# State-space decays from running sums that a DMA spreads over all partitions, in place of two TensorE products for each chunk and group

## The chip, the cores and the metric

The kernel runs on one core of one Trainium2 chip. The metric is the device time of one execution in microseconds (us). The time before is the median of three executions.

## The reference

Two layers of a decoder trunk are computed for one sequence of 1024 positions with width 1024. Each layer normalises the input, multiplies it by one input projection, feeds four branches (HGRN2, retention, Mamba-2 state space, gated linear attention), and adds the projected, gated outputs back. The change is in the state-space branch (SSD), which has 8 heads in 2 groups of 4:

```python
def chunked_scalar_decay(q, k, v, log_a):
...
    def step(state, inp):
        qc, kc, vc, ac = inp
        cum = jnp.cumsum(ac, axis=-1)
        rel = jnp.where(causal, cum[..., :, None] - cum[..., None, :], -jnp.inf)
        scores = jnp.einsum('bhtd,bhsd->bhts', qc, kc) * jnp.exp(rel)
        o = (jnp.einsum('bhts,bhsv->bhtv', scores, vc)
             + jnp.einsum('bhtd,bhdv->bhtv', qc * jnp.exp(cum)[..., None], state))
...
def ssd_branch(z_in, xbc_in, dt_in, conv_w, conv_b, dt_bias, a_log, d_skip, norm_g):
...
    dt = jax.nn.softplus(dt_in.astype(jnp.float32) + dt_bias.astype(jnp.float32)).transpose(0, 2, 1)
    a = -jnp.exp(a_log.astype(jnp.float32))
...
    y = chunked_scalar_decay(group_to_heads(cmat), group_to_heads(bmat),
                             xh * dt[..., None], dt * a[None, :, None])
```

What matters here is `exp(rel)`: for each chunk and head, a matrix over pairs of positions (s, t) with the exponential of the sum of the log decays between s and t.

## The kernel before, in words

The kernel cuts the sequence into 8 chunks of 128 positions (`NC` = 8, where the reference uses 64; the result is the same). One layer runs through its branches one after another: HGRN2 (4 heads), gated linear attention (2 pairs of heads), SSD (2 groups), retention (4 heads). Dense projections, in and out, are split in a high and a low part and take three TensorE matmuls each. They are generators, and `fill(ns)` pulls matmuls from them whenever a branch yields a number of nanoseconds: so the in-order stream of TensorE (PE) holds the small products of a branch with pieces of dense projections between them. This order is the order in which the program is written. The order on VectorE (DVE), ScalarE (ACT), GpSimd (POOL) and the DMA queue of SyncE (SP) is made by a scheduler, and each of them runs its own list strictly in order. Weights come as 256 KB slices (tile `raw`, 2 buffers) by DMAs on SP's queue; ACT rounds each to its high part (`whi`, L402), DVE makes the low part (`wlo`, L403), 4 buffers of each.

For SSD, `ssd_steps` works once in each layer, in two parts. The first computes the step sizes `dt` and the log decays `la` (128 positions of a chunk on the partitions, 8 chunks x 8 heads = 64 columns). The second, run after the HGRN2 heads, makes on PE three products of `la` with constant triangular or full matrices (L915 to L917) into one PSUM tile, takes their exponentials (L919, tile `dx`), and splits `la` into a high part `lah` and a rest `lal` (L922, L924).

`ssd_mix(l, g, ...)` works through the 8 chunks of a group; it runs four times (2 layers x 2 groups). The scores of 4 chunks at a time are 4 products on PE (`scores`, L994), masked on DVE into `M` (L997). The decay matrices of a chunk, 128 x 512 for 4 heads, come in three steps that run ahead of use:

- `factors(c)`: POOL multiplies the constant triangle `upper` by the column of `la` of each head, once for `lah` and once for `lal` (L1003, two tiles `lv`).
- `decays(c, lvs)`: PE multiplies both by the constant `after_r` into one PSUM tile `sc` (L1012, two matmuls of 512 columns), ACT takes the exponential into a tile `A` (L1014), DVE multiplies it by `M` (L1015).
- `weighted(c)`: POOL makes three scaled copies of the chunk's input (`xdt`, `xw`, `xd`, L1028).

Then PE makes the chunk's output `po` (L1061 from `A`, L1064 from the carried state; one PSUM buffer) and its state update (L1067); DVE adds them up (L1070 to L1086), ACT takes the squares (L1089). After 4 chunks POOL computes the inverse root (L269, L271), DVE scales (L1097), and PE transposes the result for the output projection (`to_feature_major`, L521). `factors` is called two chunks ahead and `decays` one chunk ahead. The tiles `lv`, `A` and `M` come from one pool of 5 buffers, `mid` (names `b2` and `lv`).

While a group runs, the dense work between its chunks is an output projection (L1118), then the convolution's projections of the next group (L417 to L419, with L946, L947 on ACT and L950 on DVE) in group 0, or the rotary projections of the retention branch (L464 to L467, with L836 on ACT and L840 to L845 on DVE and POOL) in group 1.

Of the kernel before, what the change touches and what calls it, by code (L numbers as in the profile page):

```python
# [11 lines left out]
F32 = mybir.dt.float32  # L12
F32R = mybir.dt.float32r
# [3 lines left out]
AF = mybir.ActivationFunctionType  # L17
ALU = mybir.AluOpType
MUL, ADD, SUB = ALU.mult, ALU.add, ALU.subtract
PSUM = bass.MemoryType.PSUM  # L20

P = 128
# [144 lines left out]
def hybrid_trunk(ctx, nc, tc, t_in, out, gamma_c):  # L167
    vec, act, gp, pe = nc.vector, nc.scalar, nc.gpsimd, nc.tensor
    SL = 512

    cst = ctx.enter_context(tc.tile_pool(name="cst", bufs=1))
    wp = ctx.enter_context(tc.tile_pool(name="wp", bufs=4))
    big = ctx.enter_context(tc.tile_pool(name="big", bufs=11))
    mid = ctx.enter_context(tc.tile_pool(name="mid", bufs=5))
    yp = ctx.enter_context(tc.tile_pool(name="yp", bufs=4))
    sml = ctx.enter_context(tc.tile_pool(name="sml", bufs=4))
    pp = ctx.enter_context(tc.tile_pool(name="pp", bufs=4, space=PSUM))
    pm = ctx.enter_context(tc.tile_pool(name="pm", bufs=1, space=PSUM))

    seq = [0]  # L180

    def nm(s):
        seq[0] += 1
        return f"{s}_{seq[0]}"
# [4 lines left out]
    def mid_t(n=512):  # L189
        return mid.tile([P, 512], F32, tag="b2", name=nm("b2"))[:, :n]  # L190

    def sm_t(tag, n, bufs=4, w=None):
        return sml.tile([P, w or n], F32, tag=tag, bufs=bufs, name=nm(tag))[:, :n]
# [4 lines left out]
    def ps_mix(tag, bufs=1):  # L198
        return pm.tile([P, 512], F32, tag=tag, bufs=bufs, name=nm(tag))
# [46 lines left out]
        return cols[:, o : o + n] if j is None else cols[:, o + j : o + j + 1]  # L246

    ident, upper, ones = k_("ident"), k_("upper"), k_("ones")
    after_r = cst.tile([P, P], F32R, name="after_r")
    vec.tensor_tensor(after_r, ones, upper, SUB)  # L250
    after = after_r.bitcast(F32)

    xs = cst.tile([P, NT, D], F32, name="xs")
    hh = [cst.tile([P, KT, 512], F32R, name=f"hh{i}") for i in range(2)]
# [19 lines left out]
    def bc(ap, shape):  # L274
        return ap.to_broadcast(shape)
# [603 lines left out]
    def ssd_steps(l, dl, st):  # L879
# [7 lines left out]
        def t64(tag):  # L887
            return sm_t(tag, 64, bufs=1)
# [19 lines left out]
        dt = t64("dt")  # L908
# [6 lines left out]
        pe.matmul(ps[:, 0:64], upper, la, start=True, stop=True)  # L915
        pe.matmul(ps[:, 64:128], after, la, start=True, stop=True)
        pe.matmul(ps[:, 128:192], ones, la, start=True, stop=True)  # L917
        ex = sm_t("dx", 192, bufs=1)
        act.activation(ex, ps[:, 0:192], AF.Exp)  # L919

        lah = sml.tile([P, 64], F32R, tag="lah", bufs=1, name=nm("lah"))
        vec.tensor_copy(lah, la)  # L922
        lal = t64("lal")
        vec.tensor_tensor(lal, la, lah.bitcast(F32), SUB)  # L924
        w = t64("dw")
        vec.tensor_tensor(w, ex[:, 64:128], dt, MUL)

        def v3_(a):
            return a.rearrange("p (c h) -> p c h", c=NC)

        st.update(dt=v3_(dt), la=(v3_(lah.bitcast(F32)), v3_(lal)), ec=v3_(ex[:, 0:64]), w=v3_(w),
                  dec=v3_(ex[:, 128:192]), dsk=dsk)

    def conv(l, ch, u, name):
# [50 lines left out]
    def ssd_mix(l, g, u, st, between):  # L985
# [11 lines left out]
            vec.tensor_tensor(M[half], ps.rearrange("p (c t) -> p c t", c=4), bc(upper.unsqueeze(1), [P, 4, P]), MUL)  # L997

        def factors(c):
            lvs = []  # L1000
            for part in st["la"]:
                lv = mid.tile([P, 512], F32R, tag="b2", name=nm("lv"))
                gp.tensor_tensor(lv.rearrange("p (h t) -> p h t", h=4), bc(upper.unsqueeze(1), [P, 4, P]),  # L1003
                                 bc(part[:, c, hs].unsqueeze(2), [P, 4, P]), MUL)
                lvs.append(lv)
            return lvs

        def decays(c, lvs):

            pl = ps_mix("sc", 2)  # L1010
            for i_, lv in enumerate(lvs):
                pe.matmul(pl, after_r, lv, start=(i_ == 0), stop=(i_ == 1))  # L1012
            A = mid_t().rearrange("p (h t) -> p h t", h=4)
            act.activation(A, pl.rearrange("p (h t) -> p h t", h=4), AF.Exp)  # L1014
            vec.tensor_tensor(A, A, bc(M[c // 4][:, c % 4, :].unsqueeze(1), [P, 4, P]), MUL)  # L1015
            return A

# [259 lines left out]
    for l in range(DEPTH):  # L1277
# [4 lines left out]
        st = {}  # L1282
# [176 lines left out]
```

## Time and profile before

| | |
|---|---|
| median of three executions | 2104.41 us (2104.26 to 2104.89) |
| the profiled execution, its own time | 2105.0 us |
| its span in the profile | 2103.2 us |
| mean granted TensorE clock | 0.994 |
| DMA traffic | 115.72 MB, 55 GB/s over the span |

The profile is of one execution. Its views give, for each engine, busy time and what ended each idle time (the waits), instructions in order of time (the timeline), groups by line, and busy time by stretch (windows). In the timeline a row has the start in us from the span's start, the duration of the merged instructions, engine, line, operation, tiles and count, and in brackets the idle time before it and what ended it. Matmuls are pipelined and overlap in the records: what one costs PE is the distance from its start to the start of the next. A PE product of plain 32-bit floats is recorded as two matmuls.

### The profile page before, as it was taken

How to read it: one execution, taken by the hardware profiler on the slowest of the kernel's cores; microseconds unless marked ns; L12 is line 12 of the kernel's file. 1: busy time of each engine (PE TensorE's matmuls, PEld its weight loads, DVE VectorE, ACT ScalarE, POOL GpSimd, SP SyncE). 2: the span in 40 equal slices, each digit the busy share in tenths (PEclk: the TensorE clock that was granted, in tenths of full speed). 3: DMA queues.
4: the chain of work that ended last, by engine and by line, in shares of the span. 5: the costliest groups of instructions: out<-in, count | busy, mean ns of one | idle time of the engine just before them, and what ended most of it. 6: DMA issues, size and time to landing. Idle time of an engine off the chain costs nothing.

```text
span 2103.2 us, 42832 instructions
## 1 busy us (share of the span) xinstructions
PE 2051.0 (98%) x18052; PEld 1845.4 (88%) x18052; DVE 1192.4 (57%) x2373; ACT 722.9 (34%) x1636; POOL 456.3 (22%) x628
## 2 busy tenths in 40 slices
PE   5999999999999999999999999999999999999997
PEld 4898888899888899999879888888988889999996
DVE  7656743737547476544565554465555665744456
ACT  7433223432333422222273223343234252222223
POOL 4001001011035263122220010000102526501232
PEclk9999999999999999999999999999999999999998
DMA  8233321111111111111122211111111111111112
GB/s 282 87 105 101 97 67 36 32 41 32 43 39 36 42 45 31 51 36 31 46 59 75 67 32 46 37 31 41 37 41 37 39 36 46 41 36 41 41 36 101
DMA packets 67539, 115.72 MB, mean 55 GB/s; under 512 B 9585, under 2 KB 19985, under 8 KB 67345
## 3 DMA queue, kind: packets, MB, share of 16 engines
q1 hardware_dynamic: 67056, 112.24, 17.4%
q8 instruction: 142, 2.33, 0.5%
q10 hardware_dynamic: 288, 0.73, 0.1%
q14 instruction: 53, 0.43, 0.1%
HBM read 108.75 MB, written 4.19 MB: 54 GB/s over the span
## 4 chain that ended last, share of the span: by engine, by line
PE 83%; DVE 8%; ACT 4%; DMA 2%; issue 1%; POOL 1%; SPq 0%; POOLq 0%; ACTq 0%; DVEq 0%
PE pp L1118 15%; PE pp L464 11%; PE pp L466 11%; PE pp L467 11%; PE pp L417 6%; PE pp L419 6%; PE pp L418 6%; PE ms L664 2%; PE sc L581 1%; DMA wa<-in_w_ada 1%; PE sc L521 1%; DVE b L609 1%; PE sc L668 1%; PE pp L499 1%; PE po L658 1%
## 5 line engine op out<-in xcount | busy, mean ns | idle before, releaser
L464 PE MATMUL pp<-whi,hh 128*128 128x256 f32 x2176 | 632.5, 291 | 0.7 <-ACT b L947 0.7
L467 PE MATMUL pp<-whi,hl 128*128 128x256 f32 x2176 | 615.3, 283 | 0.0
L466 PE MATMUL pp<-wlo,hh 128*128 128x256 f32 x2176 | 615.2, 283 | 0.0
L464 PEld LDWEIGHTS pp<-whi,hh 128*128 128x128 f32 x2176 | 416.7, 191 | 4.5 <-ACT b L947 1.5
L466 PEld LDWEIGHTS pp<-wlo,hh 128*128 128x128 f32 x2176 | 417.0, 192 | 0.8
L467 PEld LDWEIGHTS pp<-whi,hl 128*128 128x128 f32 x2176 | 416.5, 191 | 0.0
L402 ACT CAST whi<-raw 128x512 fp32r<-128x512 f32 x280 | 173.5, 622 | 593.5 <-PE pp L467 299.9
L403 DVE TENSOR_TENSOR wlo<-raw,whi 128x512 fp32r<-128x512 f32 x276 | 207.5, 754 | 269.9 <-ACT whi L402 257.2
L417 PE MATMUL pp<-hh,whi 128*128 128x512 f32 x640 | 270.1, 422 | 7.5 <-ACT hh L394 6.7
L419 PE MATMUL pp<-hl,whi 128*128 128x512 f32 x640 | 252.9, 395 | 1.4 <-DVE hl L395 1.4
L418 PE MATMUL pp<-hh,wlo 128*128 128x512 f32 x640 | 251.1, 392 | 0.0
L1123 DVE TENSOR_TENSOR xs<-xs,pp 128x512 f32<-128x512 f32 x256 | 173.4, 684 | 65.5 <-PE pp L1118 63.1
L1107 POOL TENSOR_TENSOR raw<-raw,gate_b 128x512 f32<-128x512 f32 x64 | 82.5, 1291 | 513.6 <-DMA raw<-in_w_out 393.5
L1118 PE MATMUL pp<-whi,yh 128*128 128x512 f32 x448 | 188.9, 422 | 0.0
L1118 PE MATMUL pp<-whi,yl 128*128 128x512 f32 x448 | 175.5, 392 | 0.0
L1118 PE MATMUL pp<-wlo,yh 128*128 128x512 f32 x448 | 175.0, 391 | 0.0
L269 POOL TENSOR_SCALAR rt<-ss 128x4 f32<-128x4 f32 (+1 forms) x46 | 12.0, 260 | 641.7 <-ACT junk L538 586.6
L419 PEld LDWEIGHTS pp<-hl,whi 128*128 128x128 f32 x640 | 120.6, 188 | 32.2 <-DVE hl L395 5.6
L417 PEld LDWEIGHTS pp<-hh,whi 128*128 128x128 f32 x640 | 121.1, 189 | 30.8 <-ACT hh L394 8.7
L418 PEld LDWEIGHTS pp<-hh,wlo 128*128 128x128 f32 x640 | 121.4, 190 | 19.3 <-DVE wlo L403 0.4
L298 DVE SCALAR_TENSOR_TENSOR b<-wa,c_act,b 128x512 f32<-128x512 f32 x84 | 71.3, 849 | 61.8 <-DMA wa<-in_w_ada 60.8
L1118 PEld LDWEIGHTS pp<-whi,yh 128*128 128x128 f32 x448 | 84.4, 188 | 20.2 <-DVE xs L1123 3.0
(242 smaller groups left out, 3182.0 us busy)
## 6 DMA issues: line engine op xcount, KB each, us to landing
raw<-in_wt SPq DMA_DIRECT2D x136, 256.0 KB, 3.0
wa<-in_w_ada SPq DMA_DIRECT2D x96, 256.0 KB, 2.9
raw<-in_wf SPq DMA_DIRECT2D x80, 256.0 KB, 2.6
raw<-in_w_out SPq DMA_DIRECT2D x64, 256.0 KB, 2.6
xs<-in_x SPq DMA_DIRECT2D x8, 512.0 KB, 7.9
out<-b SPq DMA_DIRECT2D x7, 512.0 KB, 2.6
b<-in_wt SPq DMA_DIRECT2D x4, 384.0 KB, 4.2
b<-in_rows SPq DMA_DIRECT2D x4, 256.0 KB, 3.7
```

The source lines that it names most:

```text
L298: vec.scalar_tensor_tensor(acc, w, c_act[:, k : k + 1], acc, MUL, ADD)
L402: act.copy(hi, raw)
L403: eng.tensor_tensor(lo, raw, hi.bitcast(F32), SUB)
L417: pe.matmul(ps, hi[:, j : j + P], hh[half][:, k, :], start=(k == 0), stop=False)
L418: pe.matmul(ps, lo[:, j : j + P], hh[half][:, k, :], start=False, stop=False)
L419: pe.matmul(ps, hi[:, j : j + P], hl[half][:, k, :], start=False, stop=(k == KT - 1))
L464: pe.matmul(o, hhi, hi[:, j : j + 256], start=(k == 0 and m % 2 == 0), stop=False, skip_group_check=True)
L466: pe.matmul(o, hhi, lo[:, j : j + 256], start=False, stop=False, skip_group_check=True)
L467: pe.matmul(o, hlo, hi[:, j : j + 256], start=False, stop=(k == KT - 1), skip_group_check=True)
L1107: gp.tensor_tensor(raw, raw, gate_b[:, nh * 512 : (nh + 1) * 512], MUL)
L1118: pe.matmul(ps, a[:, o : o + P], b, start=(n == 0), stop=(n == 3 * len(kts) - 1))
L1123: vec.tensor_tensor(xv, xv, ps, ADD)
```

## The change

The running sums of the log decays within a chunk are now kept themselves, in two layouts. `ssd_steps` makes with one more product (L921 of the new kernel) the sums with chunk and head on 64 partitions and position along the row, counted from the middle of the chunk by the new constant `from_mid`; DVE copies them to `cumT` (L926); PE transposes this back to positions on partitions (L927) and DVE copies that to `cum` (L928); and `cumT` is written to a tile in device memory, `cumd` (32 KB, L930). The split of `la` into `lah` and `lal` goes.

In `factors(c)` a DMA on SP's queue reads the four rows of `cumd` for the chunk and group and writes them to all 128 partitions of the tile `A` (256 KB, L1009), and POOL subtracts from each head's 128 columns the sum at the partition's own position and cuts off above zero, in place (L1011, four instructions). `decays(c, A)` is the exponential in place (L1016) and the product with `M` (L1017); the two PE matmuls, the two `lv` tiles and the PSUM tile go. `A` is thus taken from the pool `mid` two chunks ahead, not one.

```diff
+    dr = ctx.enter_context(tc.tile_pool(name="dr", bufs=1, space=bass.MemoryType.DRAM))
...
-    after_r = cst.tile([P, P], F32R, name="after_r")
-    vec.tensor_tensor(after_r, ones, upper, SUB)
-    after = after_r.bitcast(F32)
+    after = cst.tile([P, P], F32, name="after")
+    vec.tensor_tensor(after, ones, upper, SUB)
+    from_mid = cst.tile([P, P], F32, name="from_mid")
+    vec.tensor_scalar(from_mid[0:64, :], upper[0:64, :], -1.0, None, ADD)
+    vec.tensor_copy(from_mid[64:P, :], upper[64:P, :])
...
         pe.matmul(ps[:, 128:192], ones, la, start=True, stop=True)
+        pe.matmul(ps[0:64, 192:320], la, from_mid, start=True, stop=True)
         ex = sm_t("dx", 192, bufs=1)
         act.activation(ex, ps[:, 0:192], AF.Exp)
 
-        lah = sml.tile([P, 64], F32R, tag="lah", bufs=1, name=nm("lah"))
-        vec.tensor_copy(lah, la)
-        lal = t64("lal")
-        vec.tensor_tensor(lal, la, lah.bitcast(F32), SUB)
+        cum, cumT = t64("cum"), mid_t(P)[0:64, :]
+        vec.tensor_copy(cumT, ps[0:64, 192:320])
+        pe.transpose(ps[:, 320:384], cumT, ident[0:64, 0:64])
+        vec.tensor_copy(cum, ps[:, 320:384])
+        cumd = dr.tile([64, P], F32, name=f"cum{l}")
+        nc.sync.dma_start(cumd, cumT)
...
         def factors(c):
-            lvs = []
-            for part in st["la"]:
-                lv = mid.tile([P, 512], F32R, tag="b2", name=nm("lv"))
-                gp.tensor_tensor(lv.rearrange("p (h t) -> p h t", h=4), bc(upper.unsqueeze(1), [P, 4, P]),
-                                 bc(part[:, c, hs].unsqueeze(2), [P, 4, P]), MUL)
-                lvs.append(lv)
-            return lvs
-
-        def decays(c, lvs):
-
-            pl = ps_mix("sc", 2)
-            for i_, lv in enumerate(lvs):
-                pe.matmul(pl, after_r, lv, start=(i_ == 0), stop=(i_ == 1))
+
             A = mid_t().rearrange("p (h t) -> p h t", h=4)
-            act.activation(A, pl.rearrange("p (h t) -> p h t", h=4), AF.Exp)
+            r0 = c * 8 + 4 * g
+            nc.sync.dma_start(A, st["cumd"][r0 : r0 + 4, :].unsqueeze(0).to_broadcast([P, 4, P]))
+            for h in range(4):
+                gp.tensor_scalar(A[:, h, :], A[:, h, :], st["cum"][:, c, 4 * g + h : 4 * g + h + 1], 0.0, SUB, ALU.min)
+            return A
+
+        def decays(c, A):
+
+            act.activation(A, A, AF.Exp)
             vec.tensor_tensor(A, A, bc(M[c // 4][:, c % 4, :].unsqueeze(1), [P, 4, P]), MUL)
             return A
```

On PE the order differs nowhere but in the lines that go and come. At the second part of `ssd_steps` in layer 0, PE has this before (the tile `ms` is the PSUM tile of the products, `b_145` holds `la`, the rows of `pp` are the dense projection that follows):

```order
L521 MATMUL sc_4092<-cs,b_543_3991 128x128 x4
L915 MATMUL ms_4101<-b_145_1142,cs 128x64
L916 MATMUL ms_4101<-b_145_1142,after_r 128x64
L917 MATMUL ms_4101<-b_145_1142,cs 128x64
L464 MATMUL pp_3870<-whi_4049,hh_90 128x256
```

Now, at the same place (`b_556` is `cumT`; line numbers of the new kernel are 2 or 3 higher for the same code):

```order
L524 MATMUL sc_4097<-cs,b_543_3996 128x128 x4
L918 MATMUL ms_4106<-b_145_1147,cs 128x64
L919 MATMUL ms_4106<-b_145_1147,after 128x64
L920 MATMUL ms_4106<-b_145_1147,cs 128x64
L921 MATMUL ms_4106<-from_mid,b_145_1147 64x128
L927 MATMUL ms_4106<-cs,b_556_4114 128x64
L467 MATMUL pp_3875<-whi_4054,hh_95 128x256
```

Between L921 and L927 no dense work stands, and L927 reads what DVE has yet to copy from L921's output.

In layer 0, group 0, SP's queue has only weight slices before: the last slice of the output projection and the 8 slices of the convolution's projections (`in_wf`).

```order
L1106 DMA raw_7083<-in_w_out 128x512
L411 DMA raw_7258<-in_wf 128x512
L411 DMA raw_7292<-in_wf 128x512
L411 DMA raw_7351<-in_wf 128x512
L411 DMA raw_7430<-in_wf 128x512
L411 DMA raw_7522<-in_wf 128x512
```

Now the 8 loads of `A` stand among them (`cum_4118` is `cumd`; the tiles, in order, are those of chunks 0 to 7):

```order
L414 DMA raw_7259<-in_wf 128x512
L1009 DMA b_934_6930<-cum_4118 128x512
L1009 DMA b_944_6976<-cum_4118 128x512
L1009 DMA b_952_7011<-cum_4118 128x512
L1009 DMA b_963_7066<-cum_4118 128x512
L414 DMA raw_7293<-in_wf 128x512
L1009 DMA b_981_7140<-cum_4118 128x512
L414 DMA raw_7352<-in_wf 128x512
L414 DMA raw_7429<-in_wf 128x512
L1009 DMA b_995_7207<-cum_4118 128x512
L1009 DMA b_1031_7380<-cum_4118 128x512
L1009 DMA b_1043_7440<-cum_4118 128x512
```

The four loads of chunks 0 to 3 come right behind the first slice, those of chunks 5, 6 and 7 together behind the fourth. The last one takes the buffer of chunk 3, so it waits until PE has made chunk 3's `po`.

On POOL, in the same group, the inverse root of the first four chunks (`rt`, `ry`) stood behind the factors of chunk 5 (L1003) and the scaled copies of chunks 4 and 5, and ahead of the factors of chunk 6:

```order
L1003 TENSOR_TENSOR lv_7208<-cs,lah_4107 128x512
L1003 TENSOR_TENSOR lv_7210<-cs,lal_4109 128x512
L1028 TENSOR_TENSOR s_1013_7213<-b_908_6658,rbdsk_1139 128x128
L1028 TENSOR_TENSOR s_1013_7213<-b_929_6901,rbdsk_1139 128x128
L1028 TENSOR_TENSOR s_1051_7387<-b_908_6658,dt_1166 128x128
L1028 TENSOR_TENSOR s_1051_7387<-b_929_6901,dt_1166 128x128
L1028 TENSOR_TENSOR s_1053_7389<-b_908_6658,dw_4111 128x128
L1028 TENSOR_TENSOR s_1053_7389<-b_929_6901,dw_4111 128x128
L269 TENSOR_SCALAR rt_7270<-ss_6999 128x4
L271 TENSOR_TENSOR ry_7272<-rt_7270,mhalf 128x4
L1003 TENSOR_TENSOR lv_7383<-cs,lah_4107 128x512
```

Now the subtractions of chunks 5, 6 and 7 all stand ahead of it:

```order
L1011 TENSOR_SCALAR b_995_7207<-b_995_7207,cum_4113 128x128 x4
L1011 TENSOR_SCALAR b_1031_7380<-b_1031_7380,cum_4113 128x128 x4
L1030 TENSOR_TENSOR s_1032_7386<-b_908_6667,dt_1171 128x128
L1030 TENSOR_TENSOR s_1032_7386<-b_929_6910,dt_1171 128x128
L1011 TENSOR_SCALAR b_1043_7440<-b_1043_7440,cum_4113 128x128 x4
L1030 TENSOR_TENSOR s_1034_7388<-b_908_6667,dw_4120 128x128
L1030 TENSOR_TENSOR s_1034_7388<-b_929_6910,dw_4120 128x128
L272 TENSOR_SCALAR rt_7271<-ss_7008 128x4
L274 TENSOR_TENSOR ry_7273<-rt_7271,mhalf 128x4
```

So the inverse root of the first four chunks stands behind the arrival of chunk 7's load, in every group.

On DVE, in layer 0, group 1, the product with `M` of chunk 7 (L1015) stood directly ahead of the rotary products of the retention branch:

```order
L1086 TENSOR_TENSOR b_1255_8497<-b_1255_8497,b_1138_7955 128x128
L1086 TENSOR_TENSOR b_1255_8497<-b_1255_8497,b_1139_7956 128x128
L1015 TENSOR_TENSOR b_1285_8644<-b_1285_8644,b_1218_8282 128x512
L840 TENSOR_TENSOR b_1290_8666<-b_1288_8662,b_1233_8338 128x128
L841 TENSOR_TENSOR b_1290_8666<-b_1288_8662,b_1233_8338 128x128
```

Now it (L1017, second of two here, the first being chunk 6's) stands right behind the scaling of the first half (L1099), some twenty rows earlier:

```order
L1017 TENSOR_TENSOR b_1217_8486<-b_1217_8486,b_1181_8269 128x512
L1099 TENSOR_SCALAR b_1137_8073<-b_1137_8073,ry_8346 128x128 x8
L406 TENSOR_TENSOR wlo_8579<-raw_8576,whi_8578 128x512
L1017 TENSOR_TENSOR b_1226_8552<-b_1226_8552,b_1181_8269 128x512
L406 TENSOR_TENSOR wlo_8749<-raw_8746,whi_8748 128x512
```

The rotary products, and the DVE additions of chunk 6 behind them, no longer follow it.

More of the change, by code (lines that the diff above doesn't have):

```diff
@@ L929, in v3_ @@
             return a.rearrange("p (c h) -> p c h", c=NC)
-        st.update(dt=v3_(dt), la=(v3_(lah.bitcast(F32)), v3_(lal)), ec=v3_(ex[:, 0:64]), w=v3_(w),
+        st.update(dt=v3_(dt), cum=v3_(cum), cumd=cumd, ec=v3_(ex[:, 0:64]), w=v3_(w),
                   dec=v3_(ex[:, 128:192]), dsk=dsk)
```

## The prediction, made before the changed kernel ran

> **What bounds the kernel now.** I read the page's busy times first, then what TensorE (PE) waited for, then the timeline of the four stretches where the change acts.
>
> ```profile
> span 2103.2 us, 42832 instructions
> ...
> PE 2051.0 (98%) x18052; PEld 1845.4 (88%) x18052; DVE 1192.4 (57%) x2373; ACT 722.9 (34%) x1636; POOL 456.3 (22%) x628
> ```
>
> PE is busy for 2051.0 of 2103.2 us. The waits of PE, longest first:
>
> ```profile
> PE pp L377 <- DMA xs<-in_x: 13.5, 1, 13.5
> ...
> PE po L1061 <- DVE s L1079: 3.7, 4, 1.1
> ...
> PE sc L521 <- DVE b L1097: 1.1, 2, 0.5
> ```
>
> The longest is at the start, before any of this. Of the state-space stage there are 3.7 us in four waits for DVE at L1061, one in each group, and 1.1 us at L521. So PE's own list of matmuls sets the end, and a matmul that goes from a stretch without waits shortens the run by the distance between two starts. In the timeline of PE, group 0 of layer 0:
>
> ```profile
> 623.20 0.62 PE L1012 MATMUL sc<-lv,after_r 128*128 128x512 f32 x2
> 623.65 0.39 PE L1118 MATMUL pp<-whi,yh 128*128 128x512 f32 x1
> ...
> 628.87 1.00 PE L1061 MATMUL po<-s,b 128*128 128x64 f32 x8
> ...
> 649.22 0.65 PE L1064 MATMUL po<-st,b 128*128 128x256 f32 x2
> ...
> 660.40 0.60 PE L521 MATMUL sc<-cs,b 128*128 128x128 f32 x4
> ```
>
> The pair at L1012 holds PE from 623.20 to 623.65, no longer, with dense work (L1118) right behind it.
>
> **What it removes.** The group's row for these matmuls:
>
> ```profile
> L1012 PE MATMUL sc<-lv,after_r x64: 389/390/481, 623.2 to 1815.8; 128*128 128x512 f32 x64
> ```
>
> Its 390 ns is latency; the distance is 0.45 to 0.46 us for a pair, 0.455. There are 64 matmuls, 32 pairs: 32 x 0.455 = 14.6 us, all on PE's list. [...]
>
> **What it adds on PE.** Two products in each layer, in `ssd_steps`, with a round trip over DVE between them. PE and DVE there, and a plain 32-bit product elsewhere (L994, four of them in 0.81 us):
>
> ```profile
> 352.39 0.33 PE L915 MATMUL ms<-b,cs 128*128 128x64 f32 x2
> 352.56 0.39 PE L916 MATMUL ms<-b,after_r 128*128 128x64 f32 x2
> ...
> 352.98 0.36 PE L464 MATMUL pp<-whi,hh 128*128 128x256 f32 x1
> ```
>
> ```profile
> 618.20 1.06 PE L994 MATMUL sc<-b,b 128*128 128x128 f32 x8
> 619.01 0.47 PE L1118 MATMUL pp<-whi,yh 128*128 128x512 f32 x1
> ```
>
> ```profile
> 353.31 0.75 DVE L530 SCALAR_TENSOR_TENSOR yl<-sc,cols,yh 128x512 fp32r<-128x512 f32 x1 [4.44 <-ACT yh L529]
> ```
>
> ```profile
> L922 DVE CAST lah<-b x2: 186/188/189, 115.7 to 1145.2; 128x64 fp32r<-128x64 f32 x2
> ```
>
> The new product starts where L464 did, at 352.98, and takes 0.81 / 4 = 0.20 us. The transpose (L927 of the new kernel) then needs DVE's copy of it, which stands behind `yl` (L530). That ends at 353.31 + 0.75 = 354.06; the copy, at the 0.19 of L922, ends at 354.25; with about 0.1 us to hand over (an estimate) the transpose starts at 354.35 and takes the 0.17 us between L915 and L916. Dense work resumes at 354.5 instead of 352.98: 1.5 us, 3.0 in two layers. Nothing covers it, since PE's list has no dense work in between. With no wait at all it would be 2 x (0.20 + 0.17) = 0.7; with one more operation of 0.75 ahead of the copy, 2 x 2.3 = 4.6. I take 3.0, as the rows of that very place give it. DVE's second copy, the small write to memory, and the dropped split of `la` have nobody waiting within hundreds of us: the first decay matrix is wanted at 620. They count as nothing.
>
> **What it moves.** The decay matrices must reach PE in time by the new way: load, subtraction on POOL, exponential on ACT, product on DVE. Nearest rows:
>
> ```profile
> raw<-in_wf SPq DMA_DIRECT2D x80, 256.0 KB, 2.6
> ...
> xs<-in_x SPq DMA_DIRECT2D x8, 512.0 KB, 7.9
> ...
> b<-in_rows SPq DMA_DIRECT2D x4, 256.0 KB, 3.7
> ```
>
> ```profile
> 613.19 0.33 SPq L411 DMA_DIRECT2D raw<-in_wf  x1
> ```
>
> ```profile
> 620.98 1.04 POOL L1003 TENSOR_TENSOR lv<-cs,lah 128x512 fp32r<-128x512 f32 x1
> ...
> 652.21 0.86 POOL L1028 TENSOR_TENSOR s<-b,dw 128x128 f32<-128x128 f32 x2 [0.95 <-DVE b L1082]
> 653.91 0.19 POOL L269 TENSOR_SCALAR rt<-ss 128x4 f32<-128x4 f32 x1 [0.84 <-ACT junk L1089]
> 654.18 1.01 POOL L271 TENSOR_TENSOR ry<-rt,mhalf 128x4 f32<-128x4 f32 x1
> ```
>
> ```profile
> L367 POOL TENSOR_SCALAR b<-xs,ry x10: 1119/1135/1547, 18.0 to 1071.5; 128x1024 f32<-128x1024 f32 x10
> ```
>
> ```profile
> L1028 POOL TENSOR_TENSOR s<-b,dt x64: 393/399/1375, 595.4 to 1814.7; 128x128 f32<-128x128 f32 x64
> ```
>
> ```profile
> L1014 ACT ACTIVATE b<-sc x32: 575/597/604, 623.9 to 1816.9; 128x512 f32<-128x512 f32 x32
> ```
>
> ```profile
> L1015 DVE TENSOR_TENSOR b<-b,b x32: 678/775/1478, 625.8 to 1817.5; 128x512 f32<-128x512 f32 x32
> ```
>
> (In these four, behind the count: least, median and greatest ns of one.) A load takes 2.6 to 7.9 us; I take 3.7, because `b<-in_rows` is the same shape, one row of memory spread over 128 partitions. A subtraction of 128 columns is between 1135 / 8 = 142 ns and the 399 ns of a two-input one: I take 0.28, so 1.1 us for the four of a chunk (0.6 to 1.6). The first of the two `lv` products it replaces took 1.04, so POOL does no more than before.
>
> Chunk 0: SP issues its load behind the slice at 613.19, so it lands near 617.3, before POOL comes to it at 620.98 as it came to `lv`. Subtracted at 622.1, then 0.6 (L1014) and 0.8 (L1015), it is ready at 623.5; PE wants it at 628.87 less two removed pairs, 628.0. Margin 4.5 us. The load is covered by POOL's scaled copies; without that cover there would still be the 4.5.
>
> Chunk 7 has the tightest path, and not by its own use. Its load waits for PE to finish chunk 3, at 649.22 less five pairs (2.3 us), 646.9. It lands at 650.7, is subtracted by 651.8; behind it on POOL stand a copy in two parts (0.86 at 652.21) and the inverse root, 653.91 to 655.19, 1.3 us: 654.0. Then DVE scales the half (L1097):
>
> ```profile
> 655.23 1.66 DVE L1097 TENSOR_SCALAR b<-b,ry 128x128 f32<-128x128 f32 x8 [1.41 <-POOL ry L271]
> ```
>
> done at 655.7. PE comes to L521 at 660.40 - 2.3 = 658.1. Margin 2.4 us: no cost, unless the load takes over 6.1 us. The weight slices behind these loads on SP keep their time: the fifth was issued at 649.95 before (SP's row of that time, `raw<-in_wf`), three us after chunk 7's load goes out.
>
> ```profile
> 649.95 0.33 SPq L411 DMA_DIRECT2D raw<-in_wf  x1
> ```
>
> Chunks 5 to 7 are now multiplied on DVE earlier, and ACT's exponential of chunk 7 goes from the crowded end of each group. That touches the four waits at L1061:
>
> ```profile
> 680.16 0.58 ACT L1014 ACTIVATE b<-sc 128x512 f32<-128x512 f32 x1
> 680.64 0.58 ACT L946 COPY b<-pp 128x512 f32<-128x512 f32 x1
> ```
>
> ```profile
> 686.75 1.08 PE L1061 MATMUL po<-s,b 128*128 128x64 f32 x8 [0.77 <-DVE s L1079]
> ```
>
> ```profile
> 791.77 0.94 DVE L1015 TENSOR_TENSOR b<-b,b 128x512 f32<-128x512 f32 x1 [1.12 <-ACT b L1014]
> 792.64 0.28 DVE L840 TENSOR_TENSOR b<-b,b 128x128 f32<-128x128 f32 x1
> ```
>
> In group 0 the evacuation (L946, 0.48 behind the exponential), which feeds DVE's convolution ahead of L1079, starts up to 0.45 earlier. In group 1 the rotary products (L840) started 0.87 behind L1015 and can start up to 0.8 earlier without it. 2 x (0.45 + 0.8) = 2.5 of the 3.7 us go; between 0 and 3.7, and I take the 2.5 these rows give.
>
> **Sum.** -14.6 + 3.0 - 2.5 = -14.1 us. The profiled execution took 2105.0 us, 1.8 more than its span; the change touches neither its start nor its end. 2105.0 - 14.1 = 2090.9, and the median of the runs lies 0.6 under the profiled one: **2090.3 us**. Its own range: -14.6 + 0.7 - 3.7 = -17.6 to -14.6 + 4.6 - 0 = -10.0, that is 2086.8 to 2094.4.
>
> **Rivals.** *DVE becomes the bound at the end of each group.* For it, the row of the windows view for 664 to 694 us, with the five engines' busy times in the order PE, weight loads, DVE, ACT, POOL:
>
> ```profile
> 664.00:694.00 30.00, 29.23 (x149) 24.55 (x149) 26.13 (x47) 15.64 (x28) 12.39 (x18) 1.00 0.13 36
> ```
>
> DVE is busy for 26.13 of 30 us. If it sets the pace there, the three pairs of chunks 5 to 7 (3 x 4 x 0.455 = 5.5 us) and the 2.5 are not had: -6.1, 2098.3 us. Against it: three products of 0.7 leave this stretch. Chance 0.10.
>
> *Chunk 7's load comes late, and PE stands at L521.* Each us beyond the margin costs 4, once in each group. It can be mild: 1 to 2.5 us give 2094.3 to 2100.3 (chance 0.07). It can also end slower. The windows view shows what PE's clock does after a gap (after the five busy times: granted clock, DMA share, GB/s):
>
> ```profile
> 28.00:32.00 4.00, 0.18 (x2) 0.09 (x1) 3.89 (x9) 2.64 (x7) 0.00 (x0) 0.84 0.91 290
> 32.00:40.00 8.00, 7.67 (x27) 6.23 (x28) 7.79 (x7) 4.40 (x8) 6.08 (x4) 0.65 0.71 232
> ```
>
> After 3.8 us nearly idle, PE ran at 0.65 for 8 us, a loss of 0.35 x 8 = 2.8. With a wait of 3.8 in each group: -14.1 + 4 x (3.8 + 2.8) = +12.3, 2116.7 us. It decides from a landing of 3.7 + 2.4 + 3.8 = 9.9 us. For it: no load of before reads one 2 KB row of freshly written memory, with three issued together. Against: `b<-in_rows` does all but the writing at 3.7, and even 512 KB took 7.9. Chance 0.07. [...]
>
> *The removed work was covered, or does not go.* PE's list falls from 11194 rows to 11134, 64 out and 4 in, and it had no waits to cover them: 2104.4 us, chance 0.03.
>
> **Chances and range.** My forecast has 0.73. A measurement of this kernel tells 0.2%, 4.2 us, from no change. Faster by more than that: the forecast, the DVE rival and nearly all of the mild lateness, 0.89; within it, 0.04; slower, 0.07. The range for 8 in 10 is 2086.8, the forecast's low end, to 2098.5, which takes in the DVE rival and half of the mild lateness; left out are the rest of it, the slow case and no change.
>
> **What would show it.** In the profile after: no matmul reads `lv`; the distance between the neighbours of a removed pair is that of dense matmuls, 0.23; PE waits near 1.2 us for DVE at L927, twice; waits at L1061 for DVE fall under 2 us in all; the loads of `A` land in about 3.7 us and POOL needs about 1.1 us for four subtractions; L521 has no wait over 0.5 us. I am wrong if PE waits for POOL or DVE at the products of `A`, if L521 waits over 1 us in each group, or if weights (`wlo`, `whi`) come late behind the loads.

## The result and the profile after

The changed kernel takes 2118.95 us (median of 4 runs, 2114.7 to 2119.22), against 2104.43 us before (4 runs, 2104.26 to 2104.89). The ratio is 1.0066, 95% interval 1.0053 to 1.0078: slower by 14.5 us where 14.1 us of gain were forecast. The profiled execution has a span of 2117.0 us (2103.2 before), 13.8 us more.

The page of the changed kernel first. PE is busy for 5.4 us less than before and a longer span, so time went into waiting:

```profile
span 2117.0 us, 42883 instructions
...
PE 2045.6 (97%) x17994; PEld 1840.3 (87%) x17994; DVE 1176.5 (56%) x2375; ACT 719.9 (34%) x1632; POOL 475.6 (22%) x692
```

What PE waited for (line numbers stand two or three higher than before: L524 is the old L521, L1063 the old L1061):

```profile
PE sc L524 <- DVE b L1099: 12.3, 6, 2.9
...
PE po L1063 <- DVE b L1078: 5.2, 4, 1.3
...
PE ms L927 <- DVE b L926: 3.5, 2, 1.8
...
PE po L1063 <- DVE s L1081: 1.5, 2, 0.8
```

L524 went from 1.1 to 12.3 us. The four waits at L1063 for DVE's scaling L1081 fell from 3.7 to 1.5 us in total (the two of group 0 are gone, the two of group 1 went from about 1.05 to 0.77 us each), but a new one of 1.3 us stands in each group at the same line, for DVE's addition L1078. The subtraction and the load, by their lines (least, median and greatest ns of one; then the load's median from issue to landing, 3.6 us):

```profile
L1011 POOL TENSOR_SCALAR b<-b,cum x128: 703/710/1219, 624.1 to 1811.6; 128x128 f32<-128x128 f32 x128
```

```profile
b<-cum SPq DMA_DIRECT2D x32, 256.0 KB, 3.6
```

The loads are what the prediction took them for (3.7). The subtraction is not: by the median it takes 0.71 us for one head and 2.84 for a chunk, and with the longer ones counted 3.1 for a chunk (99.6 us of POOL for 32 chunks), where 0.28 and 1.1 were taken. POOL's timeline at the end of the first half of group 0 in layer 0, two of ACT's rows there, and PE's row behind them:

```profile
651.89 0.76 POOL L1030 TENSOR_TENSOR s<-b,rbdsk 128x128 f32<-128x128 f32 x2 [2.17 <-PE po L1063]
652.62 6.21 POOL L1011 TENSOR_SCALAR b<-b,cum 128x128 f32<-128x128 f32 x8
...
659.54 3.15 POOL L1011 TENSOR_SCALAR b<-b,cum 128x128 f32<-128x128 f32 x4
...
663.85 0.19 POOL L272 TENSOR_SCALAR rt<-ss 128x4 f32<-128x4 f32 x1 [0.43 <-ACT junk L1091]
664.13 1.03 POOL L274 TENSOR_TENSOR ry<-rt,mhalf 128x4 f32<-128x4 f32 x1
```

```profile
662.73 0.63 ACT L1016 ACTIVATE b<-b 128x512 f32<-128x512 f32 x1 [2.72 <-POOL b L1011]
663.27 0.40 ACT L1091 ACTIVATE junk<-b 128x256 bf16<-128x256 f32 x1
```

```profile
665.54 1.11 PE L524 MATMUL sc<-cs,b 128*128 128x128 f32 x4 [2.64 <-DVE b L1099]
```

POOL works without a pause from 651.89 to 663.42: the subtractions of chunks 5 and 6 (6.21), those of chunk 7 (3.15), copies between them, and only then the inverse root, which before ended at 655.19 and now ends at 665.16. Its last wait, of 0.43 us, is for ACT: the squares of chunk 3 (L1091), which the root needs, stand in ACT's list behind the exponential of chunk 7 (L1016), and that waits for POOL's last subtraction. So the subtractions hold the root up in two ways at once, and the root in another place of POOL's list alone would still have waited for those squares. DVE's scaling L1099 waits for the root, PE for the scaling.

The other new wait, at the start of the same group. The rows are POOL's, ACT's, DVE's and PE's, each from its own timeline:

```profile
624.12 11.78 POOL L1011 TENSOR_SCALAR b<-b,cum 128x128 f32<-128x128 f32 x16
```

```profile
635.92 0.63 ACT L1016 ACTIVATE b<-b 128x512 f32<-128x512 f32 x1 [2.22 <-POOL b L1011]
```

```profile
636.59 0.93 DVE L1017 TENSOR_TENSOR b<-b,b 128x512 f32<-128x512 f32 x1 [1.37 <-ACT b L1016]
637.44 0.41 DVE L1078 TENSOR_TENSOR b<-po,s 128x256 f32<-128x256 f32 x1
```

```profile
638.00 1.08 PE L1063 MATMUL po<-s,b 128*128 128x64 f32 x8 [1.32 <-DVE b L1078]
```

Four chunks of subtractions in a row take 11.78 us. The fourth chunk's exponential, and with it DVE's product, comes at 636.59; chunk 0's addition L1078 is queued behind that product on DVE, and it frees the PSUM tile (`po`) that PE's next products need.

Last, the clock. The windows view (PE, weight loads, DVE, ACT, POOL; then granted clock, DMA share, GB/s), first a short window at the wait at L524, then the stretches with new waits:

```profile
664.00:667.00 3.00, 1.46 (x6) 1.32 (x7) 1.80 (x9) 0.58 (x2) 1.08 (x2) 0.70 0.00 0
```

```profile
340.00:380.00 40.00, 38.24 (x229) 31.60 (x228) 18.99 (x33) 20.61 (x32) 3.77 (x4) 0.96 0.10 28
600.00:720.00 120.00, 115.67 (x671) 101.27 (x670) 71.05 (x129) 43.65 (x82) 58.90 (x91) 0.99 0.19 56
735.00:830.00 95.00, 89.44 (x623) 83.59 (x623) 61.72 (x145) 27.17 (x59) 59.88 (x97) 0.98 0.19 57
1360.00:1400.00 40.00, 38.24 (x282) 35.87 (x280) 11.87 (x30) 14.32 (x35) 7.55 (x8) 0.96 0.11 33
1640.00:1730.00 90.00, 86.06 (x481) 74.85 (x480) 53.50 (x106) 29.87 (x60) 46.23 (x78) 0.98 0.21 60
1765.00:1850.00 85.00, 79.99 (x547) 74.53 (x546) 54.97 (x131) 23.50 (x56) 56.70 (x95) 0.98 0.22 66
```

Before, the clock is 1.00 in all six. Length times what is missing: 1.6 + 1.2 + 1.9 + 1.6 + 1.8 + 1.7 = 9.8 us. The sum for the profiled execution is then -14.6 (products gone) + 3.5 + 0.7 (waits and products at L921 to L927) + 11.2 (L524) + 5.2 - 2.2 (L1063) + 9.8 (clock) = 13.6, of 13.8 measured. That it comes so close is partly luck: a clock given to two places leaves about 2 us open over these 470 us, from 1850 us on the clock was a little higher than in the kernel before (0.99 against 0.98), and the mean clock of the whole executions (0.991 and 0.994) speaks of some 6 us, not 9.8. That wait and clock together make the loss is shown; their shares are not known to the microsecond.

### The profile page after: what moved, and what is told of

Its sections match the earlier page's. It is cut to its first block, busy times and chain, and to the rows that moved or that the text cites. A ratio compares the mean times of both kernels' runs of the same rounds, so it can differ in the third digit from the quotient of the medians.

```text
span 2117.0 us, 42883 instructions
## 1 busy us (share of the span) xinstructions
PE 2045.6 (97%) x17994; PEld 1840.3 (87%) x17994; DVE 1176.5 (56%) x2375; ACT 719.9 (34%) x1632; POOL 475.6 (22%) x692
## 4 chain that ended last, share of the span: by engine, by line
PE 79%; DVE 8%; ACT 4%; POOL 4%; DMA 2%; issue 2%; SPq 0%; POOLq 0%; ACTq 0%; DVEq 0%
PE pp L1120 13%; PE pp L467 11%; PE pp L469 11%; PE pp L470 11%; PE pp L420 6%; PE pp L422 6%; PE pp L421 6%; POOL b L1011 3%; DMA wa<-in_w_ada 2%; PE ms L667 2%; PE sc L524 1%; PE sc L584 1%; DVE b L612 1%; PE po L1063 1%; PE sc L671 1%
## 5 line engine op out<-in xcount | busy, mean ns | idle before, releaser
L406 DVE TENSOR_TENSOR wlo<-raw,whi 128x512 fp32r<-128x512 f32 x276 | 201.3, 732 | 281.2 <-ACT whi L405 268.3
```

The costliest lines, as they stand in the source:

```text
L406: eng.tensor_tensor(lo, raw, hi.bitcast(F32), SUB)
```

## The experiments

The theory: POOL's subtraction costs 0.71 us and not 0.28; through POOL's list, which is worked off in order, it delays the inverse root (L524) and DVE's additions (L1063); and a wait of PE can also cost clock (1.76 us at L927 and 2.64 to 2.95 at L524, in stretches with 0.96 to 0.99). The rivals: the loads or SP's order are at fault; DVE's order, which the scheduler changed, is at fault; a wait costs only its own length.

### The price of the subtraction (e1_forms)

```diff
-            for h in range(4):
-                gp.tensor_scalar(A[:, h, :], A[:, h, :], st["cum"][:, c, 4 * g + h : 4 * g + h + 1], 0.0, SUB, ALU.min)
+            if c % 2 == 0:
+                gp.tensor_scalar(A[:, 0, :], A[:, 0, :], col_[0], 0.0, SUB, ALU.min)
+                gp.tensor_scalar(A[:, 1, :], A[:, 1, :], col_[1], None, SUB)
+                gp.tensor_scalar(A[:, 2, :], A[:, 2, :], col_[2], 0.0, MUL, ADD)
+                gp.tensor_scalar(A[:, 3, :], A[:, 3, :], col_[3], 0.0, SUB, ADD)
+            else:
+                gp.tensor_scalar(A[:, 0, :], A[:, 0, :], col_[0], 0.0, ADD, ALU.min)
+                gp.tensor_scalar(A[:, 1, :], A[:, 1, :], col_[1], None, MUL)
+                gp.tensor_scalar(A[:, 2, :], A[:, 2, :], 0.5, 0.0, SUB, ALU.min)
+                gp.tensor_tensor(A[:, 3, :], A[:, 3, :], bc(col_[3], [P, P]), SUB)
...
-            act.activation(A, A, AF.Exp)
+            act.activation(A, A, AF.Exp, scale=0.0)
```

> Measures the disputed price by itself. Each of the 128 subtractions of 128 columns on POOL stands in one of eight forms (even chunks: subtract and minimum as in the change; subtract alone; multiply and add zero; subtract and add zero. Odd chunks: add and minimum; multiply alone; subtract and minimum with two constants; a two-input subtraction from the column spread out). The exponential is taken with scale 0, so the decays are left out of the result. If POOL is slow with subtraction or minimum as operations, the multiply-and-add form takes 0.14 to 0.3 us and the form of the change 0.71. If it is slow with any operation of one input that reads its scalar from a column, all six such forms take about 0.7 and the one with two constants less. If only size counts (a fixed part of 0.57 us), all take about 0.7, the two-input form too. Total time: 2110 to 2119 us.

This run and the next leave the decays out of their result: the exponential takes its input times zero. The eight forms are L1012 to L1015 and L1017 to L1020, in the order of the diff, with 16 operations of each. The lines view has them by cost (busy us of all 16 and mean ns of one behind the bar):

```profile
L1013 POOL TENSOR_SCALAR b<-b,cum 128x128 f32<-128x128 f32 x16 | 14.7, 920 | 0.0
L1017 POOL TENSOR_SCALAR b<-b,cum 128x128 f32<-128x128 f32 x16 | 14.4, 900 | 0.0
...
L1019 POOL TENSOR_SCALAR b<-b 128x128 f32<-128x128 f32 x16 | 11.8, 739 | 0.0
...
L1012 POOL TENSOR_SCALAR b<-b,cum 128x128 f32<-128x128 f32 x16 | 11.5, 722 | 0.0
L1015 POOL TENSOR_SCALAR b<-b,cum 128x128 f32<-128x128 f32 x16 | 11.5, 721 | 0.0
...
L1018 POOL TENSOR_SCALAR b<-b,cum 128x128 f32<-128x128 f32 x16 | 10.5, 654 | 0.0
L1014 POOL TENSOR_SCALAR b<-b,cum 128x128 f32<-128x128 f32 x16 | 8.0, 500 | 0.0
L1020 POOL TENSOR_TENSOR b<-b,cum 128x128 f32<-128x128 f32 x16 | 6.4, 400 | 0.0
```

Multiply-and-add, the form of L367 from which the prediction took its lower end, is the fastest form of one input: 0.50 us on the mean, from 0.38 to 0.63 in POOL's timeline of 620 to 660 us. Subtract-and-minimum and subtract-and-add need 0.72 on the mean, add-and-minimum as much in three of its four rows in that timeline (1.16 in the fourth); one operation alone needs 0.61 at least there, and a subtraction alone 0.92 on the mean; constants in place of a column save nothing (0.74). The two-input subtraction with the column spread out takes 0.40, less than any of these means, and no row there is over 0.41. Some forms take very different times at different places (0.62 to 1.11 us for the subtraction alone); why was not tried. So none of the three expected patterns holds alone: the pair multiply-and-add is a case of its own, and "one input is cheaper than two" is wrong for the pair that the change uses. With 2.8 us of POOL for a chunk (88.8 us for 32) this run took 2104.72 us (one run), 14 less than the change and below the expected 2110 to 2119: its six waits at L524 are 9.1 us in all, the longest 2.2, and of the stretches of the four groups only one has a clock under 1.00 (0.98 from 1765 to 1850 us).

### No subtraction, loads kept (e2_nosub)

```diff
-            for h in range(4):
-                gp.tensor_scalar(A[:, h, :], A[:, h, :], st["cum"][:, c, 4 * g + h : 4 * g + h + 1], 0.0, SUB, ALU.min)
...
-            act.activation(A, A, AF.Exp)
+            act.activation(A, A, AF.Exp, scale=0.0)
```

> The changed kernel with the subtractions on POOL left out (the exponential takes its input with scale 0, so the decays are left out of the result); the loads stay as they are. POOL's price as the cause: the waits at L524 (12.3 us) and those on the chain of chunk 0's additions at L1063 (5.2 us) go, and with them the clock lost behind L524; what stays is -14.6 for the products and about +7.5 for the two round trips in the first products (3.5 of waits, 0.7 of products, 3.3 of clock), with 0 to -3.7 at L1063: 2093.5 to 2098 us, I take 2096. The loads or SP's order as the cause: the waits at L524 stay, 2114 to 2119 us.

2096.64 us (5 runs, 2096.12 to 2097.76), ratio to before 0.9963 (0.995 to 0.9975). What PE waited for:

```profile
PE ms L927 <- DVE b L926: 3.5, 2, 1.8
...
PE sc L524 <- DVE b L1097: 1.1, 2, 0.6
```

L524 is back at 1.1 us and the wait for chunk 0's addition is gone, with every load in place. The loads are not at fault, and POOL's subtractions are needed for both waits. DVE's order isn't the cause at L1063 either: the product of chunk 3 still stands ahead of that addition in DVE's list here.

### One two-input subtraction for a chunk (e3_onesub)

```diff
-            for h in range(4):
-                gp.tensor_scalar(A[:, h, :], A[:, h, :], st["cum"][:, c, 4 * g + h : 4 * g + h + 1], 0.0, SUB, ALU.min)
+            gp.tensor_tensor(A, bc(st["cum"][:, c, hs].unsqueeze(2), [P, 4, P]), A, SUB)
...
-            act.activation(A, A, AF.Exp)
+            act.activation(A, A, AF.Relu)
+            act.activation(A, A, AF.Exp, scale=-1.0)
```

> The changed kernel with one two-input subtraction of 128 x 512 on POOL for each chunk in place of four of 128 columns, and the cutoff at zero on ACT (a Relu of the difference ahead of the exponential, which then has scale -1), so the same result. POOL then needs about 1.04 us for each chunk, as for one scaled copy of before, close to the 1.1 of my prediction. POOL's price as the cause: 2093.5 to 2099 us, I take 2097. The loads as the cause: 2114 to 2119 us. If the cutoff on ACT (some 0.6 us for each chunk) now holds up the products instead, waits at L1063 stay and it is 2100 to 2106.

2096.27 us (5 runs, 2094.44 to 2098.05), ratio 0.996 (0.9947 to 0.9972). POOL's timeline at the place of the late inverse root:

```profile
649.22 2.04 POOL L1010 TENSOR_TENSOR b<-cum,b 128x512 f32<-128x512 f32 x2
...
652.57 1.08 POOL L1010 TENSOR_TENSOR b<-cum,b 128x512 f32<-128x512 f32 x1
...
654.80 0.40 POOL L272 TENSOR_SCALAR rt<-ss 128x4 f32<-128x4 f32 x1 [0.20 <-ACT junk L1091]
```

Chunks 5 to 7 take 3.1 us in place of 9.4, and the root starts at 654.80, nine us earlier than in the change, two of them because this run reaches the group earlier (its first copies there start at 619.72, the change's at 621.85). At the price that the prediction had assumed (1.05 us for a chunk), the same transfers, with the subtractions of three chunks still ahead of the root, gain time: 8.4 us against the before of the same session. That is the step that failed. It is not all of the miss: the run stays 6 us over the 2090.3 that was forecast. The uncovered round trip below explains 3 to 4.5 of them (1.2 more of waits and products than forecast, and 1.6 to 3.3 of clock); the rest is open.

### More work on POOL, known to the scheduler (e7_twoops, e8_threeops)

```diff
             gp.tensor_tensor(A, bc(st["cum"][:, c, hs].unsqueeze(2), [P, 4, P]), A, SUB)
+            gp.tensor_tensor(A, A, bc(ones[:, 0:4].unsqueeze(2), [P, 4, P]), MUL)
+            gp.tensor_tensor(A, A, bc(ones[:, 0:4].unsqueeze(2), [P, 4, P]), MUL)
```

The diff is to e3_onesub; e7_twoops has the first of the two products, e8_threeops both.

> The run with one two-input subtraction for each chunk on POOL and the cutoff on ACT, with a second two-input operation of 128 x 512 on POOL behind it (a product with ones; the same result): 2.09 us of POOL for each chunk, between the 1.05 of that run and the 2.84 of the change. If POOL's list has a margin at the inverse root, as the prediction argued, that 2.84 overruns: 3 x 0.75 less than the change behind chunk 4 leaves about 0.4 us of the 2.64 us waits at L524: 2096 to 2100 us. If the time goes in proportion to POOL's work: 2109.5. If what counts is where the scheduler put DVE's products (they stand later in this run's order than in the change's), 2096 to 2098.

> As the run with two operations, with three: 3.14 us of POOL for each chunk, over the 2.84 of the change, while the scheduler knows of it and has put DVE's products of A later in its list than in the change. POOL's price as the cause of the waits at L524: they come back at 2.6 to 3.5 us in each group; with the clock lost behind them 2113 to 2124 us. DVE's order as the cause, made by a scheduler that took the subtractions for cheap: no waits at L524 over 1 us, 2096 to 2100.

e7_twoops: 2100.38 us (11 runs, 2099.64 to 2102.22), ratio 0.9982 (0.9974 to 0.9991). e8_threeops: 2140.36 us (5 runs, 2138.06 to 2142.7), ratio 1.0171 (1.0158 to 1.0185). PE's waits, of the first and then of the second:

```profile
PE sc L524 <- DVE b L1100: 4.9, 6, 1.0
```

```profile
PE sc L524 <- DVE b L1101: 18.0, 6, 4.3
...
PE po L1065 <- POOL s L1032: 7.1, 4, 1.8
```

The two-operation run lies 0.4 us above the range expected of a margin that is just overrun (waits of up to 1.0 us, not 0.4), and nine us under the proportion. The waits at L524 come back with three operations although DVE's products stand later in its list: it is POOL's time, not DVE's order. That run overshot its range (2124) by 16 us, for a reason that no theory had named: POOL's scaled copies, which PE's products read directly, came late too (L1065 for POOL, 7.1 us), and PE stood more often with less clock (0.94 to 0.96 in the windows of all four groups). The scheduler also interleaved POOL's list otherwise there: one product of chunk 7 stands between the two steps of the root.

Together the runs give time against POOL's busy time on these lines for a chunk, as the profiled executions show it (the lists differ too, as said): 0 us, 2096.6; 1.0, 2096.3; 2.3, 2100.4; 2.8, 2104.7 (a single run); 3.1, 2118.95; 3.4, 2140.4. Nothing is lost up to 1.0, a little at 2.3, and more with every step above: a margin that is used up, not a slope.

### The round trip in the first products (e4_spaced, e5_roundtrip)

e4_spaced is the changed kernel with other units' products between the first new product and the transpose:

```diff
         vec.tensor_copy(cumT, ps[0:64, 192:320])
+        yield 3000
         pe.transpose(ps[:, 320:384], cumT, ident[0:64, 0:64])
...
-        for _ in steps:
-            pass
+        run(steps)
```

> The changed kernel with 3 us of out-projection products of other units placed between the first new product and the transpose behind it, so that DVE's copy is covered in each layer; nothing else is changed. If a wait costs its own length alone: the 3.5 us of waits at L927 go, 2115.4 us. If each of those two waits also halves the clock for some 3.4 us: another 3.3 go, 2112.1 us, and the granted clock between 340 and 380 us is 1.00 in place of 0.96.

e5_roundtrip is the kernel before with these additions alone:

```diff
         pe.matmul(ps[:, 128:192], ones, la, start=True, stop=True)
+        pe.matmul(ps[0:64, 192:320], la, from_mid, start=True, stop=True)
...
+        cum, cumT = tmp[:, 320:384], mid_t(P)[0:64, :]
+        vec.tensor_copy(cumT, ps[0:64, 192:320])
+        pe.transpose(ps[:, 320:384], cumT, ident[0:64, 0:64])
+        vec.tensor_copy(cum, ps[:, 320:384])
```

> The kernel before with one part of the change alone: the two new products of the first products' stage in each layer, with DVE's copy between them (the running sums go unused; nothing is left out). My prediction's term, 3.0 us, would give 2107.4. With the waits that the changed kernel showed there (3.5) and the products (0.7), but no loss of clock: 2108.6. With a loss of some 1.65 us of clock behind each of the two waits as well: 2111.9, and the granted clock falls behind 352 us in the windows view. If the clock falls behind only one of them in an execution, 2110.3.

e4_spaced: 2112.48 us (6 runs, 2110.77 to 2115.64), ratio to before 1.0036 (1.0024 to 1.0049), 6.5 us under the change. e5_roundtrip: 2109.22 us (8 runs, 2106.76 to 2112.13), ratio 1.0024 (1.0014 to 1.0034), 4.7 us over the kernel before. The windows view of 340 to 380 us, covered (e4_spaced) and then uncovered (e5_roundtrip):

```profile
340.00:380.00 40.00, 40.00 (x249) 32.98 (x249) 20.70 (x35) 22.27 (x34) 3.78 (x4) 1.00 0.10 28
```

```profile
340.00:380.00 40.00, 38.24 (x233) 31.71 (x232) 18.44 (x32) 19.84 (x31) 3.79 (x4) 0.96 0.09 27
```

The trace shows the loss of clock behind the wait plainly. In the medians it is less sharp: covering the copy gave 6.5 us where the waits alone are 3.5, adding it cost 4.7 where waits and products alone are 4.2; the runs of e5_roundtrip spread from 2106.8, under the sum without a loss of clock (2108.7), to the sum with two (2112). So the loss comes in some executions and not in others.

### Both causes removed (e6_bias_spaced), and the pairs put back (e9_pairs)

```diff
-            for h in range(4):
-                gp.tensor_scalar(A[:, h, :], A[:, h, :], st["cum"][:, c, 4 * g + h : 4 * g + h + 1], 0.0, SUB, ALU.min)
...
-            act.activation(A, A, AF.Exp)
+            for h in range(4):
+                act.activation(A[:, h, :], A[:, h, :], AF.Relu, bias=st["cum"][:, c, 4 * g + h : 4 * g + h + 1], scale=-1.0)
+            act.activation(A, A, AF.Exp, scale=-1.0)
...
         vec.tensor_copy(cumT, ps[0:64, 192:320])
+        yield 3000
...
-        for _ in steps:
-            pass
+        run(steps)
```

> The changed kernel with no subtraction on POOL: ACT takes the difference and the cutoff (a Relu for each head with the column as its bias, then one exponential with scale -1; the same result), and with the copy in the first products covered as in the spaced run. If POOL's price and the uncovered copy with their loss of clock are the whole of what went wrong, what is left is -14.6 + 0.7, and 0 to -3.7 at L1061: 2086.8 to 2091, I take 2090. If the loads cost anything besides, it stays over 2095. If ACT's five operations for each chunk (about 1.6 us) come too late for the products, waits at the products of A for DVE grow over 2 us each and it is 2095 to 2102.

2089.29 us (5 runs, 2086.95 to 2090.5), ratio to before 0.9929 (0.9916 to 0.9941). It beats both kernels, by 15 and by 30 us. Its waits and ACT's groups (busy us and mean ns behind the bar):

```profile
PE po L1064 <- DVE s L1082: 1.5, 2, 0.8
...
PE sc L524 <- DVE b L1100: 1.2, 2, 0.6
```

```profile
L1016 ACT ACTIVATE b<-b,cum 128x128 f32<-128x128 f32 x128 | 41.0, 393 | 3.6 <-DMA b<-cum 3.5
L1017 ACT ACTIVATE b<-b 128x512 f32<-128x512 f32 x32 | 20.0, 624 | 0.3
```

ACT now spends (41.0 + 20.0) / 32 = 1.9 us on a chunk, more than the 1.6 that the author had estimated, and PE does not wait for it: its waits at these lines are those of e2_nosub within 0.1 us, where nothing is subtracted. ACT is busy for 36% of this run and has no inverse root in its list.

e9_pairs puts 32 pairs of products back into this kernel, in `decays`, where the removed ones stood:

```diff
         def decays(c, A):
+            pl = ps_mix("sc", 2)
+            for i_ in range(2):
+                pe.matmul(pl, hh[0][:, 0, 0:P], hh[0][:, 0, :], start=(i_ == 0), stop=(i_ == 1))
```

> The run without subtractions on POOL and with the covered copy, with 32 pairs of products of 128 x 512 put back at the places of the removed ones (they read slices of the normalized input that are long there, and nothing reads what they write; the result is the same). It measures the term -14.6 by itself: 2089.3 + 14.6 = 2103.9 us if each pair holds TensorE for 0.455 us with nothing else to cover; 2089 to 2095 if the stretch is paced by another engine and the pairs fit beside it. A few us under 2103.9 (down to 2101) if they move the work so that the waits at L1061 change as predicted.

2102.22 us (11 runs, 2100.43 to 2104.19), ratio 0.9986 (0.9977 to 0.9995). That is 12.9 us over e6_bias_spaced by the medians (12.5 when each is taken against the before of its own session) and 14.7 by the spans of the profiled executions (2102.1 and 2087.4; the first is one of the slower of its 11). The pairs were on the path that sets the end.

## Why the prediction was wrong, point by point

**The step that failed** is the price of the subtraction: "A subtraction of 128 columns is between 1135 / 8 = 142 ns and the 399 ns of a two-input one: I take 0.28". It took 710 ns by the median, outside both ends. The lower end scaled a multiply-and-add of 1024 columns down to 128; the same form at 128 columns takes 0.38 to 0.63 us in the timeline of e1_forms, and subtract-and-minimum is not that form. The upper end assumed that one input can't cost more than two; it costs 1.8 times as much. The rows of before held no one-input subtraction and no minimum on POOL, so the bound should have stood open to above, and the range with it. At this size the runs show no fixed order between one input and two on POOL: 0.40 us for two inputs, 0.38 at least for multiply-and-add, 0.71 for subtract-and-minimum.

**The margin for chunk 7**, 2.4 us, hung on that price and on a place in POOL's list. The prediction let POOL come to chunk 7 as soon as its load had landed. In fact the subtractions of chunks 5 and 6 stand behind a scaled copy that waits for PE (651.89 in the changed kernel), so that those of three chunks, 3 x 2.84 = 8.5 us and more, fall between that copy and the root. At 0.28 for each they would have been 3.4 us and would have fitted, as e3_onesub shows with 3.1. The prediction had chunk 7 subtracted by 651.8 and the root done at 654.0; it was subtracted at 662.69 and the root done at 665.16. "POOL does no more than before" read the first of two `lv` products only: both together took 2.4 us for a chunk (78.0 us for 32), so that 3.1 is not much more. What is new is the place: in layer 0 before, no product of `lv` stood between that copy and the root, now three chunks of subtractions do. The cause is thus the price in this place; no run kept the price and changed the place. That the load must stay under 6.1 us was the wrong thing to watch.

**Chunk 0's margin**, 4.5 us, held for its own product; what came late was DVE's addition behind the product of chunk 3, after 11.78 us of subtractions. The prediction looked at when each matrix is wanted and not at what is queued behind it on DVE.

**The removed products**, -14.6: right within some 2 us; e9_pairs gives 12.5 to 14.7.

**The round trip**, +3.0: the waits and products came to 4.2, inside the range of 0.7 to 4.6. The copy did not wait for `yl` but for ACT. The rows of ACT and DVE of the changed kernel, the first with the load of a table ahead of the exponential:

```profile
352.34 1.28 ACT L923 ACT_TABLE_LOAD   x1
353.63 0.33 ACT L923 ACTIVATE dx<-ms 128x192 f32<-128x192 f32 x1
```

```profile
352.35 0.75 DVE L533 SCALAR_TENSOR_TENSOR yl<-sc,cols,yh 128x512 fp32r<-128x512 f32 x1 [4.44 <-ACT yh L532]
353.99 0.28 DVE L926 COPY b<-ms 64x128 f32<-64x128 f32 x1 [0.89 <-ACT dx L923]
```

`yl` ended at 353.10, the copy started at 353.99, when ACT had read the same PSUM tile (`ms`). The 0.1 us to hand over to PE was the author's estimate and had no row; here the copy ended at 354.27 and the transpose started at 354.33. Left out altogether was the clock behind the wait: the prediction charged clock to a gap in a rival only, and nothing to its own wait, taken as 1.2 us and measured as 1.76.

**The waits at L1061**, -2.5: 3.7 became 1.5, so -2.2. The total is partly luck: group 0 gave 1.6 where 2 x 0.45 = 0.9 was forecast, group 1 gave 0.5 where 2 x 0.8 = 1.6 was. **The loads**, 3.7: 3.6.

**The rivals.** The one that ended slower had the right end of the chain, PE standing at the transposes (L521) once in each group with a loss of clock behind it, but laid it on the load; waits of 2.6 to 2.9 us came from POOL instead. It gave 2116.7 us a chance of 0.07, and 2118.95 was measured. That its number is near is luck. It put the price of the clock at a gap of 3.8 us; gaps of 1.8 us were enough in 11 of 14 cases. DVE as the bound at the end of a group did not show: in e3_onesub and e6_bias_spaced the time is had.

With no subtraction on POOL and the copy covered, what is left of the forecast's own sum holds: -14.6 + 0.7 - 2.5 = -16.4 foretold, -15.3 measured in e6_bias_spaced against the before of its session. (The forecast's 2090.3 still held 3.0 for the uncovered copy; that 2089.3 lies so near it is chance.)

## What to carry to other kernels

An operation that the trace of before does not show, on an engine that works its list off in order, has no upper bound from its neighbours (here 0.71 us, where 0.40 was taken for the upper end): leave the price open, and ask first what is queued behind it there. Move small arithmetic to the engine that has room at that place of its list (here ACT's bias), and put other work between the halves of a round trip of PE. A wait on the engine that sets the end can be worth more than its length: behind 1.76 us of it the granted clock here was 0.51 for 3.5 us.

## What the runs showed of the hardware

- POOL, 128 x 128 in 32 bits, means of 16 in e1_forms: two-input subtraction 0.40 us, multiply-and-add 0.50 (0.38 at least in the timeline of 620 to 660 us), multiplication alone 0.65 (0.61 at least there) and subtraction alone 0.92 (0.62), subtract-and-minimum and subtract-and-add 0.72; 128 x 512 of two inputs 1.05 us for the four heads together (e3_onesub), where four subtract-and-minimum took 2.84.
- A gap of 1.76 us on PE halved its clock for some 3.5 us (granted 0.51 from 354.50 to 358.00, 1.00 from 358.00 to 360.00). PE's rows behind the wait at L927 in the changed kernel; the starts of 256-column products lie 0.21 us apart, and 0.12 again from 358.06 on:

```profile
354.33 0.27 PE L927 MATMUL ms<-cs,b 64*128 64x64 f32 x1 [1.76 <-DVE b L926]
...
357.47 0.41 PE L469 MATMUL pp<-wlo,hh 128*128 128x256 f32 x1
357.68 0.42 PE L470 MATMUL pp<-whi,hl 128*128 128x256 f32 x1
...
358.06 0.28 PE L469 MATMUL pp<-wlo,hh 128*128 128x256 f32 x1
358.17 0.28 PE L470 MATMUL pp<-whi,hl 128*128 128x256 f32 x1
```

- It does not happen each time. In seven profiled executions with this same gap in both layers, the clock fell behind 11 of the 14 gaps and stayed at 1.00 behind three. Of the four longer waits at L524, all four cost clock in the changed kernel (2.64 to 2.95 us; 0.72 to 0.76 granted in the 6 or 7 us around them) and three in e4_spaced (3.0 at most; 0.98 to 0.99 over their stretches); of those in e1_forms (2.2 at most), one. The stretch in e4_spaced with no loss (the changed kernel has 0.98 in the same stretch, with PE busy for 89.44 us):

```profile
735.00:830.00 95.00, 89.36 (x630) 83.24 (x629) 62.58 (x146) 28.38 (x62) 60.00 (x97) 1.00 0.19 54
```

- Behind the four waits of 1.3 us at L1063 in the changed kernel the clock stayed at 1.00. Where the limit lies, and what decides in a single execution, was not tried.
